# Seven products in the down projection, weight sums by accumulating DMA, whole-unit low parts and a wide input projection, in a one-core macaron block

## The chip, the cores and the metric

The kernel runs on one core of a Trainium2 chip. The metric is the device time of one execution in microseconds. The kernel before took 1792.8 us (median of 3 runs, 1792.15 to 1795.28). One further execution was profiled; everything that is said of stages and instructions comes from that one.

## What is computed

One layer for 256 tokens of width 2048, in float32: a half-step SwiGLU FFN (hidden width 5632), a mixer with two head groups, a second half-step FFN, and a final norm.

```python
x = x + 0.5 * swiglu_ffn(rms_norm(x, ffn1_norm), wg1, wu1, wd1)
z = rms_norm(x, mix_norm) @ w_in                  # 2048 -> 5120
lru_x, lru_gate, sc_b, sc_c, sc_x = split(z, 1024)
h = rg_lru(conv4(lru_x), ...)                     # gates, scan over the 256 tokens
y = concat(rms_norm(h * gelu(lru_gate)), rms_norm(sc_b * conv3(sc_c * sc_x)))
x = x + y @ w_out
x = x + 0.5 * swiglu_ffn(rms_norm(x, ffn2_norm), wg2, wu2, wd2)
out = rms_norm(x, final_norm)
# swiglu_ffn(x, g, u, d) = (silu(x @ g) * (x @ u)) @ d
```

## The kernel before

**Precision.** Every large product is taken in three matmuls on float32r operands. A value v is split into hi (a rounded copy, made by ScalarE) and lo = v - hi (made by VectorE), for weights and activations alike, and hi x hi, lo x hi and hi x lo are added in PSUM. A weight *unit* is a block of 512 rows by 512 columns, loaded by one 1 MB DMA into a tile of 128 x 4 x 512 (`load`, line 155). `parts_of` (line 169) makes its parts in two halves of 128 x 1024 each: hi, then lo, of one half, then of the other. The hi and lo tiles of a half come from a pool of three; inside an FFN two more sets lie in an extra pool.

**Products.** `multiply` (line 197) runs 24 matmuls of 512 columns per unit for both token tiles: all with the weight's hi, then all with its lo. `product` (line 289) is a plain product over units into two PSUM banks. `columns` (line 271) is the input projection: there the weight columns are stationary, and the moving operand is the activation, of which hi lies in columns 0 to 255 of a tile and lo in columns 256 to 511. For each of 4 rows of blocks j and 4 column blocks f it issues three matmuls of 256 columns: hi x hi, hi x lo, lo x hi.

**Seven products.** For gate and up in an FFN, `seven` (line 350) takes two units of K and two units of columns, with the two token tiles, as a 2 x 2 by 2 x 2 block product and does it with 7 products instead of 8 (Strassen in Winograd's form). Each product is one set of 12 matmuls. The other two units of K are added in the plain way (`usual`). The order on TensorE is p0, p4, x(2,1), p5, x(3,1), p6, p2, x(2,0), p3, x(3,0), p1. The products need four sums of weight units: w12 - w11, then w22 - that (both in the tile of w11), w22 - w12, and the second minus w21. VectorE forms all four, on tiles of 128 x 2048. The tiles of w11 and w12 come from a "kept" pool of two, the other six loads go through `raws`, a pool of three. The sums of activations (`seven_of`, line 333) are made once per FFN, and their tiles `vs` hold the same two kept buffers until then. 20 sevens run in all: five for gate and five for up in each FFN.

**Order of an FFN** (`ffn`, line 401): a plain gate product for the first 512 hidden columns, the norm's factor, a plain up product while the parts of x are made, then for s = 0 to 4 a gate seven and an up seven, and after s = 0, 2 and 4 a *down part* (`down`, line 468): four plain products, one per 512 output columns, over the 3, 4 and 4 hidden units that are ready. In FFN 1 the first product is `opening` (line 533): it works through each unit j by j, needing hi and lo of a j together, and turns x meanwhile; inside it the instructions of VectorE, ScalarE and TensorE keep the program's order. Elsewhere a scheduler orders the instructions of each engine when the program is built, and the order is fixed from then on. Each engine executes its own list in that order. All weight loads are issued by SP, in its list's order, and wait there for their buffer.

**Mixer.** `columns` runs ten times; after each of its units a few deferred pieces of element-wise work (convolutions, gates, roots, reciprocals, scan, GeLU) are issued (`pump`). The functions `lru_x`, `lru_gate`, `sc_c`, `sc_x` and `sc_b` take the product from PSUM. Outside the FFNs there is no extra pool.

Of the kernel before, what the change touches and what calls it, by code (L numbers as in the profile page):

```python
# [16 lines left out]
P = 128  # L17
D = 2048
S = 256
# [29 lines left out]
def hybrid_block(ctx: ExitStack, tc: tile.TileContext, a: dict, out: bass.AP):  # L49
# [26 lines left out]
    splits = ctx.enter_context(tc.tile_pool(name="splits", bufs=3))  # L76
# [92 lines left out]
    def parts_of(raw, name, pieces=((0, UK),), split=None):  # L169
        parts = []  # L170
        for h in range(2):
            pool, bufs = splits, 3
            if extra:
                turn_of["split"] += 1
                if turn_of["split"] % 5 > 2:
                    pool, bufs = extra[0], 2
            hi = pool.tile([P, 2, CW], F32R, tag="hi", name=f"hi_{name}_{h}", bufs=bufs)
            lo = pool.tile([P, 2, CW], F32R, tag="lo", name=f"lo_{name}_{h}", bufs=bufs)
            for i, e in pieces:
                if split and i // 2 == h:  # L180
                    split(i)
                o = slice(max(i - 2 * h, 0), min(e - 2 * h, 2))
                if o.start < o.stop:
                    r = raw[:, 2 * h + o.start : 2 * h + o.stop, :]
                    act.copy(hi[:, o, :], r)
                    dve.tensor_tensor(lo[:, o, :], r, f32(hi[:, o, :]), op=ALU.subtract)
            parts.append((hi, lo))
        return [(parts[j // 2][0][:, j % 2, :], parts[j // 2][1][:, j % 2, :]) for j in range(UK)]

    def unit(src, name, pieces=((0, UK),), loaded=None, split=None):  # L190
        return parts_of(load(src, name, pieces, loaded, None), name, pieces, split)
# [119 lines left out]
    class Seven:  # L311
        def __init__(self, name):
            self.tiles = [big(f"sf_{name}_{i}") for i in range(4)]

        def part(self, i):
            o = i % 2 * S
            tile = self.tiles[i // 2][:, :, o : o + S]
            return tile[:, :, :P], tile[:, :, P:]

        def blocks(self, i):  # L320
            hi, lo = self.part(i)
            return [(hi[:, j, :], lo[:, j, :]) for j in range(UK)]

        def put(self, i, v, minus=False):
            hi, lo = self.part(i)
            if minus:
                act.activation(hi, v, AF.Copy, scale=-1.0)
                dve.scalar_tensor_tensor(lo, v, -1.0, f32(hi), op0=ALU.mult, op1=ALU.subtract)
            else:
                act.copy(hi, v)  # L330
                dve.tensor_tensor(lo, v, f32(hi), op=ALU.subtract)

    def seven_of(name, v0, v1, spare):

        sf = Seven(name)
        a11, a21, a12, a22 = v0[:, :, :P], v0[:, :, P:], v1[:, :, :P], v1[:, :, P:]
        sf.put(0, a11)
        dve.tensor_tensor(spare, a21, a22, op=ALU.add)
        sf.put(4, spare)
        dve.tensor_tensor(a21, a11, a21, op=ALU.subtract)  # L340
        dve.tensor_tensor(a11, spare, a11, op=ALU.subtract)
        sf.put(5, a11)
        sf.put(6, a21)
        sf.put(1, a12)
        dve.tensor_tensor(a12, a12, a11, op=ALU.subtract)
        sf.put(2, a12)
        sf.put(3, a22, True)
        return sf

    def seven(w, c0, sf, xp, name, keep, between=None):  # L350
# [3 lines left out]
        def get(u, n, kept=False):  # L354
            src = w[u * UK * P : (u + 1) * UK * P, c0 + n * CW : c0 + (n + 1) * CW]
            return load(src, f"{name}_{u}{n}", kept=kept)

        w11, w12 = get(0, 0, True), get(0, 1, True)
        b2, w22, b3, a2, w21, a3 = get(2, 1), get(1, 1), get(3, 1), get(2, 0), get(1, 0), get(3, 0)
# [6 lines left out]
        def strassen(i, raw, ps, begin=False, end=True):  # L366
            multiply([(ps, sf.blocks(i), begin, end)], parts_of(raw, f"{name}_p{i}"), True)

        def usual(u, raw, n, *targets):

            blk = parts_of(raw, f"{name}_x{u}{n}")
            multiply([(ps, stationary(xp[u - 2], t), b, e) for ps, t, b, e in targets], blk, True)

        strassen(0, w11, a, True)
# [4 lines left out]
        usual(2, b2, 1, (e, 1, True, False), (c, 0, False, False))  # L379
        dve.tensor_tensor(w11, w22, w11, op=ALU.subtract)  # L380
        strassen(5, w11, a)
# [3 lines left out]
        usual(3, b3, 1, (e, 1, False, True), (c, 0, False, False))  # L385
        dve.tensor_tensor(w12, w22, w12, op=ALU.subtract)
        strassen(6, w12, a)
        u3 = snap(a, "u3")
        strassen(2, w22, c)
        usual(2, a2, 0, (d, 0, True, False), (a, 1, False, False))  # L390
        dve.tensor_tensor(w11, w11, w21, op=ALU.subtract)
        strassen(3, w11, a, end=False)
        usual(3, a3, 0, (a, 1, False, True), (d, 0, False, False))
        strassen(1, w21, d)
# [6 lines left out]
    def ffn(tag, norm, after, opening=None):  # L401
        with tc.tile_pool(name=f"ffn{tag}", bufs=1) as fp:
# [4 lines left out]
            def keep(name):  # L407
                return fp.tile([P, CW], F32, tag="keep", name=name, bufs=12)

            hidden = {}  # L410
            waiting = []

            def turn_hidden(u, t, h):
# [10 lines left out]
                dve.tensor_tensor(lo, pt, f32(hi), op=ALU.subtract)  # L424

# [23 lines left out]
            xp = []  # L449
            for u in (0, 1, 2, 3):  # L450
                x = f32(norm.xT[u])
                dve.tensor_tensor(vs[u], x[:, :, :S], x[:, :, S:], op=ALU.add)
                dve.tensor_tensor(vs[u], vs[u], bcs, op=ALU.mult)
                if u == 1:
                    sf = seven_of(f"x{tag}", vs[0], vs[1], keep(f"spare{tag}").rearrange("p (j c) -> p j c", j=UK))
                if u > 1:
                    xp.append(big(f"xp{tag}_{u}"))
                    act.copy(xp[-1][:, :, :S], vs[u])
                    dve.tensor_tensor(xp[-1][:, :, S:], vs[u], f32(xp[-1][:, :, :S]), op=ALU.subtract)
            pu = product(wu, 0, range(4), norm.xT.__getitem__, f"u{tag}_0")  # L460
            for t in range(NT):
                dve.scalar_tensor_tensor(sg[t], pu[t], norm.r[:, t : t + 1], sg[t], op0=ALU.mult, op1=ALU.mult)
                waiting.append((0, t, sg[t]))
# [4 lines left out]
            def down(last):  # L468
                us = sorted(set(hidden) | {w[0] for w in waiting})
                for c in range(NC_D):  # L470
# [4 lines left out]
                    for t in range(NT):  # L475
                        xr = xres[:, t, c * CW : (c + 1) * CW]
                        Engine.pinned = end
                        dve.scalar_tensor_tensor(xr, ps[t], 0.5, xr, op0=ALU.mult, op1=ALU.add)
                        if last:
                            after(c, t)  # L480
                hidden.clear()

            for s in range(5):
                c0 = CW + 2 * s * CW
                g = seven(wg, c0, sf, xp, f"g{tag}_{s}", keep, settle)
                for q in ((1, 1), (0, 1), (1, 0), (0, 0)):
# [4 lines left out]
                    else:  # L491
                        act.activation(g[q], g[q], AF.Silu)
                h = seven(wu, c0, sf, xp, f"u{tag}_{s}", keep)
                for t, n in ((1, 1), (0, 1), (1, 0), (0, 0)):
                    dve.tensor_tensor(g[t, n], h[t, n], g[t, n], op=ALU.mult)
                    waiting.append((1 + 2 * s + n, t, g[t, n]))
# [36 lines left out]
    def opening(wg):  # L533

        ps = [bank(f"ps_g1_0_{t}") for t in range(NT)]
        for u in range(KD // UK):
            src = wg[u * UK * P : (u + 1) * UK * P, :CW]
            if u == 0:
                blk = unit(
                    src, "g1_0_0", ((0, 1), (1, 2), (2, 4)),  # L540
                    lambda i: load_x(1) if i == 1 else None,
                    lambda i: n1.turn((i,) if i < 2 else (2, 3)),
                )
# [32 lines left out]
    with tc.tile_pool(name="mixer", bufs=1) as mp, tc.tile_pool(name="mixw", bufs=2) as mw:  # L576
# [129 lines left out]
        def lru_gate(ps, half):  # L706
            for f in range(4):
                q = 4 * half + f
                g = tmp("g", q, bufs=4)
                dve.tensor_tensor(g, ps[f][:, :S], bc, op=ALU.mult)  # L710
# [3 lines left out]
        def sc_c(ps, half):  # L714
            for f in range(4):
# [3 lines left out]
                act.copy(c[:, 2:], ps[f][:, :S])  # L719
                cc[q] = c  # L720

        def sc_x(ps, half):
            for f in range(4):
                q = 4 * half + f
                c = cc[q][:, 2:]
                dve.tensor_tensor(c, ps[f][:, :S], c, op=ALU.mult)
# [130 lines left out]
```

## Time and profile before

| what | value |
|---|---|
| median of 3 runs | 1792.8 us |
| the profiled execution | 1791.42 us |
| its span (first to last instruction) | 1789.6 us |
| mean granted TensorE clock | 0.997 |
| instructions | 22287 |
| matmuls | 8743 |
| HBM read | 339.82 MB |

The page gives busy time by engine, a chain followed back from the last instruction, and groups of equal instructions. TensorE has two rows: PE for the matmul itself and PEld for loading the stationary operand, which runs beside it. Names in the groups are those of tiles without their numbers: ps_d is a down product's bank, ps_g_a bank a of a gate seven, hi_in and lo_in the parts of an input projection unit. A table by stage, from a query by windows, is shown where it is used; the stages are the opening and the up product (0 to 66 us), a gate and an up seven with a down part of three units (to 217), four sevens and a down part of four units (to 475), the same again (to 733), the input projection (to 973), the output projection (to 1064), and FFN 2 (to 1790).

### The profile page before, as it was taken

What the parts mean: (1) busy time and instruction counts of PE and PEld (TensorE: products, weight loads), DVE (VectorE), ACT (ScalarE), POOL (GpSimd) and SP (SyncE); (2) the same over time, 40 slices, a digit from 0 to 9 for tenths busy, and PEclk for the clock granted to TensorE, in tenths of its full rate; (3) what the DMA queues carried; (4) which work ended last, traced back from release to release, by engine and by line L of the source; (5) the groups of instructions that cost most, each with busy time, mean ns of one, the idle gap of its engine ahead of it and who ended that gap; (6) DMA issues with size and microseconds to landing.
All of it is one profiled execution on the core that took longest, in us unless ns stands there. A gap on an engine that the chain in (4) does not pass through costs nothing.

```text
span 1789.6 us, 22287 instructions
## 1 busy us (share of the span) xinstructions
PE 1765.3 (99%) x8743; PEld 1482.6 (83%) x8743; DVE 1366.0 (76%) x1448; ACT 969.6 (54%) x1204; POOL 6.9 (0%) x32
## 2 busy tenths in 40 slices
PE   7999999999999999999999999999999999999998
PEld 6788888888888888999999887888888888888886
DVE  7996689874789865587886778885889855899854
ACT  6664355653466654465655455653556633656543
POOL 1000000000000000000000000000000000000000
PEclk9999999999999999999999999999999999999999
DMA  7466456575465665455555565575565655555751
GB/s 260 165 213 234 142 190 210 188 250 194 142 203 190 215 230 179 133 172 187 173 182 188 184 203 190 176 258 175 178 205 194 213 191 185 188 188 189 242 205 70
DMA packets 173913, 343.35 MB, mean 192 GB/s; under 512 B 5620, under 2 KB 8048, under 8 KB 173680
## 3 DMA queue, kind: packets, MB, share of 16 engines
q1 hardware_dynamic: 173344, 340.82, 56.1%
q8 instruction: 68, 1.11, 0.3%
q10 hardware_dynamic: 144, 1.05, 0.1%
q14 instruction: 37, 0.30, 0.0%
q0 software_dynamic: 320, 0.07, 0.0%
HBM read 339.82 MB, written 2.10 MB: 191 GB/s over the span
## 4 chain that ended last, share of the span: by engine, by line
PE 92%; DVE 4%; issue 1%; ACT 1%; DMA 1%; SPq 0%; DVEq 0%; ACTq 0%
PE ps_d L42 27%; PE ps_in L42 13%; PE ps_g_a L42 9%; PE ps_u_a L42 9%; PE ps_g_c L42 6%; PE ps_o L42 5%; PE ps_u_c L42 5%; PE ps_u_d L42 5%; PE ps_g_d L42 3%; PE ps_g_e L42 3%; PE ps_u_e L42 2%; PE ps_u L42 2%; PE ps_g L42 2%; DVE raw_u L42 1%; PE ph L42 1%
## 5 line engine op out<-in xcount | busy, mean ns | idle before, releaser
L42 PE MATMUL ps_d<-hi_d,h 128*128 128x512 f32 x1408 | 339.2, 393 | 0.2
L42 DVE TENSOR_TENSOR lo_d<-raw_d,hi_d 128x1024 fp32r<-128x1024 f32 x176 | 210.0, 1221 | 154.9 <-PE ps_d L42 135.6
L42 ACT CAST hi_d<-raw_d 128x1024 fp32r<-128x1024 f32 x176 | 176.8, 1048 | 251.0 <-PE ps_d L42 225.4
L42 PEld LDWEIGHTS ps_d<-hi_d,h 128*128 128x128 f32 x1408 | 263.7, 188 | 58.9 <-ACT h L42 0.8
L42 PE MATMUL ps_in<-xT_nm,hi_in 128*128 128x256 f32 x1280 | 231.4, 283 | 0.0
L42 ACT CAST hi_g_p<-raw_g 128x1024 fp32r<-128x1024 f32 x140 | 142.4, 1050 | 108.4 <-DVE raw_g L42 59.5
L42 PEld LDWEIGHTS ps_in<-xT_nm,hi_in 128*128 128x128 f32 x1280 | 199.6, 192 | 0.2
L42 DVE TENSOR_TENSOR lo_u_p<-raw_u,hi_u_p 128x1024 fp32r<-128x1024 f32 x140 | 166.4, 1219 | 37.6 <-issue 16.9
L42 ACT CAST hi_u_p<-raw_u 128x1024 fp32r<-128x1024 f32 x140 | 143.6, 1047 | 87.1 <-DVE raw_u L42 45.5
L42 DVE TENSOR_TENSOR lo_g_p<-raw_g,hi_g_p 128x1024 fp32r<-128x1024 f32 x140 | 166.3, 1218 | 24.7 <-PE ps_d L42 12.4
L42 PE MATMUL ps_in<-xT_nm,lo_in 128*128 128x256 f32 x640 | 181.1, 283 | 0.0
L42 PE MATMUL ps_d<-lo_d,h 128*128 128x512 f32 x704 | 175.6, 391 | 0.0
L42 PEld LDWEIGHTS ps_d<-lo_d,h 128*128 128x128 f32 x704 | 132.2, 188 | 28.8
L42 DVE TENSOR_TENSOR lo_in<-raw_in,hi_in 128x1024 fp32r<-128x1024 f32 x80 | 97.2, 1217 | 46.8 <-ACT hi_in L42 43.3
L42 ACT CAST hi_in<-raw_in 128x1024 fp32r<-128x1024 f32 x80 | 83.6, 1047 | 84.0 <-PE ps_in L42 74.4
L42 PEld LDWEIGHTS ps_in<-xT_nm,lo_in 128*128 128x128 f32 x640 | 122.7, 192 | 0.0
L42 ACT CAST hi_u_x<-raw_u 128x1024 fp32r<-128x1024 f32 x80 | 82.7, 1051 | 52.2 <-PE ps_u_a L42 17.6
L42 ACT CAST hi_g_x<-raw_g 128x1024 fp32r<-128x1024 f32 x80 | 82.8, 1049 | 43.9 <-PE ps_g_a L42 16.7
L42 DVE TENSOR_TENSOR lo_g_x<-raw_g,hi_g_x 128x1024 fp32r<-128x1024 f32 x80 | 95.8, 1218 | 3.0 <-ACT hi_g_p L42 1.2
L42 DVE TENSOR_TENSOR lo_u_x<-raw_u,hi_u_x 128x1024 fp32r<-128x1024 f32 x80 | 96.0, 1218 | 2.0 <-ACT hi_u_p L42 0.7
L42 DVE TENSOR_TENSOR raw_g<-raw_g,raw_g 128x2048 f32<-128x2048 f32 x40 | 91.3, 2287 | 5.6 <-DMA raw_g<-in_ffn_w_gate_dram 5.2
L42 DVE TENSOR_TENSOR raw_u<-raw_u,raw_u 128x2048 f32<-128x2048 f32 x40 | 91.4, 2285 | 0.8 <-DMA raw_u<-in_ffn_w_up_dram 0.4
(273 smaller groups left out, 2766.4 us busy)
## 6 DMA issues: line engine op xcount, KB each, us to landing
raw_u<-in_ffn_w_up_dram SPq DMA_DIRECT2D x88, 1024.0 KB, 5.4
raw_d<-in_ffn_w_down_dram SPq DMA_DIRECT2D x88, 1024.0 KB, 5.1
raw_g<-in_ffn_w_gate_dram SPq DMA_DIRECT2D x87, 1024.0 KB, 5.2
raw_in<-in_w_in_dram SPq DMA_DIRECT2D x40, 1024.0 KB, 5.2
raw_o<-in_w_out_dram SPq DMA_DIRECT2D x16, 1024.0 KB, 5.1
xres<-in_x_dram SPq DMA_DIRECT2D x4, 512.0 KB, 8.0
fin<-in_final_norm_dram ACTq DMA_DIRECT2D x1, 1024.0 KB, 8.0
out_dram<-xres SPq DMA_DIRECT2D x4, 256.0 KB, 2.6
```

The lines of the kernel that those rows point to most:

```text
L42: ins = getattr(self.engine, name)(*args, **kwargs)
```

## The change

1. **Seven products in the down parts.** Of the four output column blocks, c = 0 and 3 stay plain products. Blocks 1 and 2 are done by one `seven` over the last two hidden units (m, n); the other one or two units are added in the plain way. The activation's parts for it are made in each down part from copies of the turned hidden tiles (`turned`), with tiles from the `keep` pool (13 buffers instead of 12).
2. **Two of four weight sums by DMA.** In every seven, t1 = w12 + w11 and t3 = w12 + w22 are formed by loading w12 into a kept tile (twice) and adding w11 or w22 to it by an accumulating DMA on the POOL queue. The signs of the second column are turned to allow for sums in place of differences. So t1 and t3 hold the kept tiles, w11 goes through `raws`, and a seven has 11 transfers of 1 MB in place of 8. The other two sums stay on VectorE, as additions into t1.
3. **Whole-unit parts.** hi and lo are tiles of a whole unit; hi is still written in two halves, lo in one instruction of 128 x 2048 after both. The pool holds two units, the extra pool of an FFN one more. Only the first unit of the opening keeps its pieces.
4. **Wide input projection.** hi of the weights meets hi and lo of the activation in one matmul of 512 columns; the bank's second half is added to the first when it is taken out (`halves`, a ScalarE copy, and an addition on VectorE).
5. x's parts are made for all four units (`xs`), and the scratch of the POOL queue's DMAs is 2048 bytes instead of 8192.

The core of the diff:

```diff
-    splits = ctx.enter_context(tc.tile_pool(name="splits", bufs=3))
+    splits = ctx.enter_context(tc.tile_pool(name="splits", bufs=2))
...
+    def parts_of(raw, name, pieces=((0, 2), (2, UK)), split=None, minus=False):
+        pool, bufs = splits, 2
+        if extra:
+            turn_of["split"] += 1
+            if turn_of["split"] % 3 == 0:
+                pool, bufs = extra[0], 1
+        hi = pool.tile([P, UK, CW], F32R, tag="hi", name=f"hi_{name}", bufs=bufs)
+        lo = pool.tile([P, UK, CW], F32R, tag="lo", name=f"lo_{name}", bufs=bufs)
+        for i, e in pieces:
+            if split:
+                split(i)
+            if minus:
+                act.activation(hi[:, i:e, :], raw[:, i:e, :], AF.Copy, scale=-1.0)
+            else:
+                act.copy(hi[:, i:e, :], raw[:, i:e, :])
+            if split:
+                dve.tensor_tensor(lo[:, i:e, :], raw[:, i:e, :], f32(hi[:, i:e, :]), op=ALU.subtract)
+        if minus:
+            dve.scalar_tensor_tensor(lo, raw, -1.0, f32(hi), op0=ALU.mult, op1=ALU.subtract)
+        elif not split:
+            dve.tensor_tensor(lo, raw, f32(hi), op=ALU.subtract)
+        return [(hi[:, j, :], lo[:, j, :]) for j in range(UK)]
...
-                    pe.matmul(ps[f][:, :S], hi[:, fs], x[:, :S], start=begin, stop=False)
-                    pe.matmul(ps[f][:, :S], hi[:, fs], x[:, S:], start=False, stop=False)
+                    pe.matmul(ps[f], hi[:, fs], x, start=begin, stop=False)
                     pe.matmul(ps[f][:, :S], lo[:, fs], x[:, :S], start=False, stop=end)
...
+        def sum_of(u, n, u1, n1):
+            raw = load(at(u, n), f"{name}_s{u}{n}{u1}{n1}", kept=True)
+            nc.gpsimd.dma_start(raw, at(u1, n1).rearrange("(j p) c -> p j c", p=P), accum_op=ALU.add)
+            return raw
+        (r0, r1), two = rows, len(xs) > 1
+        w11, t1, t3 = get(r0, 0), sum_of(r0, 1, r0, 0), sum_of(r0, 1, r1, 1)
+        b2, w22 = get(xs[0][0], 1), get(r1, 1)
...
-        dve.tensor_tensor(w11, w12, w11, op=ALU.subtract)
-        strassen(4, w11, c, True)
+        product_of(4, t1, c, True)
...
+                for c in (0, 3):
...
+                    if c == 0:
+                        m, n = us[-2:]
+                        sh = seven_of(
+                            hidden[m], hidden[n], {(t, i): turned[u, t] for t in range(NT) for i, u in ((0, m), (1, n))},
+                            quad(keep(f"hspare{tag}_{m}")),
+                            [[quad(keep(f"hs{tag}_{m}_{i}_{z}", F32R)) for z in range(2)] for i in range(4)],
+                        )
+                        q = seven(wd, (m, n), CW, sh, [(u, hidden[u]) for u in us[:-2]], f"d{tag}_{m}", keep)
+                        for c1 in (1, 2):
+                            for t in range(NT):
+                                update(c1, t, q[t, c1 - 1], (0.5, -0.5)[c1 - 1])
...
+        def halves(ps, name):
+            b = tmp("half", name, bufs=4)
+            act.copy(b, ps[:, S:])
+            return b
...
-                dve.tensor_tensor(z[:, 3:], ps[f][:, :S], bc, op=ALU.mult)
+                b = halves(ps[f], f"x{q}")
+                dve.tensor_tensor(b, ps[f][:, :S], b, op=ALU.add)
+                dve.tensor_tensor(z[:, 3:], b, bc, op=ALU.mult)
```

More of the change, by code (lines that the diff above doesn't have):

```diff
@@ L167, in load, with unit @@
         return raw
[L169 to L191, printed above, removed]
+    def parts_of(raw, name, pieces=((0, 2), (2, UK)), split=None, minus=False):
[20 more added lines that the diff above has]
+        return [(hi[:, j, :], lo[:, j, :]) for j in range(UK)]
+    def unit(src, name):
+        return parts_of(load(src, name, kept=None), name)
     def stationary(tile, t):
@@ L333, in seven_of @@
[L333 to L347, printed above, removed]
-        return sf
@@ L352, in seven, with quad, at, get @@
+    def quad(tile):
+        return tile.rearrange("p (j c) -> p j c", j=UK)
+    def seven(w, rows, c0, sf, xs, name, keep, between=None):
         a, c, e, d = (bank(f"ps_{name}_{n}") for n in "aced")
[L354 to L359, printed above, removed]
+        def at(u, n):
+            return w[u * UK * P : (u + 1) * UK * P, c0 + n * CW : c0 + (n + 1) * CW]
+        def get(u, n):
+            return load(at(u, n), f"{name}_{u}{n}")
+        def sum_of(u, n, u1, n1):
[5 more added lines that the diff above has]
+        b2, w22 = get(xs[0][0], 1), get(r1, 1)
+        b3 = get(xs[1][0], 1) if two else None
+        a2, w21 = get(xs[0][0], 0), get(r1, 0)
+        a3 = get(xs[1][0], 0) if two else None
@@ L384, in seven @@
             between()
-        usual(3, b3, 1, (e, 1, False, True), (c, 0, False, False))
-        dve.tensor_tensor(w12, w22, w12, op=ALU.subtract)
-        strassen(6, w12, a)
+        if two:
+            usual(1, b3, 1, (e, 1, False, True), (c, 0, False, False))
+        product_of(6, t3, a)
         u3 = snap(a, "u3")
[L389 to L394, printed above, removed]
+        product_of(2, w22, c)
+        usual(0, a2, 0, (d, 0, True, False), (a, 1, False, False))
+        dve.tensor_tensor(t1, w21, t1, op=ALU.add)
+        product_of(3, t1, a, end=not two)
+        if two:
+            usual(1, a3, 0, (a, 1, False, True), (d, 0, False, False))
+        product_of(1, w21, d)
         dve.tensor_tensor(u3, u3, s5, op=ALU.add)
@@ L469, in down, with update @@
                 us = sorted(set(hidden) | {w[0] for w in waiting})
-                for c in range(NC_D):
+                def update(c, t, ps, factor=0.5):
+                    xr = xres[:, t, c * CW : (c + 1) * CW]
+                    Engine.pinned = last and tag == 2 and c == NC_D - 1
+                    dve.scalar_tensor_tensor(xr, ps, factor, xr, op0=ALU.mult, op1=ALU.add)
+                    if last:
+                        after(c, t)
+                for c in (0, 3):
                     end = last and tag == 2 and c == NC_D - 1
@@ L538, in opening @@
             if u == 0:
[L539 to L543, printed above, removed]
+                pieces = ((0, 1), (1, 2), (2, 4))
+                raw = load(src, "g1_0_0", pieces, lambda i: load_x(1) if i == 1 else None)
+                blk = parts_of(raw, "g1_0_0", pieces, lambda i: n1.turn((i,) if i < 2 else (2, 3)))
             else:
```

118 lines of the change are left out of this document (65 added, 53 removed).

## Prediction

> **What bounds the kernel now.** I read the page first (busy shares, chain), then a table by stage, then who made TensorE wait, and last the groups by form for the price of one instruction.
>
> ```profile
> PE 1765.3 (99%) x8743; PEld 1482.6 (83%) x8743; DVE 1366.0 (76%) x1448; ACT 969.6 (54%) x1204; POOL 6.9 (0%) x32
> ...
> q1 hardware_dynamic: 173344, 340.82, 56.1%
> ...
> PE 92%; DVE 4%; issue 1%; ACT 1%; DMA 1%; SPq 0%; DVEq 0%; ACTq 0%
> ```
>
> TensorE is busy in 1765.3 of 1789.6 us and carries 92% of the chain, so the time falls only by less work on TensorE or by fewer of the 24.3 us in which it idles. The table by stage (length, then busy us of PE, PEld, DVE, ACT, POOL, granted clock, DMA share, GB/s) shows what stands close behind it: opening, four sevens, a down part, the input projection, the start of FFN 2, the tail.
>
> ```profile
> 0.00:66.00 66.00, 55.89 (x243) 44.33 (x243) 52.07 (x76) 41.84 (x70) 5.89 (x16) 0.97 0.68 240
> ...
> 217.40:392.90 175.50, 175.19 (x778) 142.50 (x777) 156.24 (x138) 106.13 (x122) 0.00 (x0) 1.00 0.59 204
> 392.90:475.40 82.50, 82.50 (x361) 67.57 (x361) 42.70 (x41) 29.98 (x32) 0.00 (x0) 1.00 0.54 179
> ...
> 733.00:973.30 240.30, 240.30 (x1993) 239.48 (x1992) 182.40 (x274) 135.91 (x203) 1.05 (x16) 1.00 0.55 180
> ...
> 1110.00:1204.70 94.70, 92.07 (x410) 74.23 (x408) 83.71 (x73) 56.79 (x66) 0.00 (x0) 1.00 0.62 213
> ...
> 1698.30:1789.60 91.30, 82.60 (x361) 67.26 (x359) 45.45 (x61) 35.71 (x52) 0.00 (x0) 0.97 0.40 139
> ```
>
> In the sevens DVE runs at 156.24 of 175.5 us (89%), and still TensorE loses only 0.3 us there. The granted clock is 1.00 in the stages shown but the first and the last, so it is no term. The waits of TensorE are few:
>
> ```profile
> PE ps_g_c L42 <- ACT hi_g_p L42: 4.3, 2, 2.5
> PE pb_n L42 <- DVE diag_n L42: 2.8, 1, 2.8
> ...
> PE ps_g L42 <- DVE lo_g L42: 1.9, 3, 0.8
> PE ps_u_a L42 <- ACT hi_u_p L42: 0.9, 5, 0.3
> ```
>
> So relieving DVE can win 0.9 us in the sevens; the gain must come from the matmuls.
>
> **Part 1: fewer matmuls.** The chain's long pieces give the spacing of a matmul:
>
> ```profile
> 875.48 97.90 PE ps_in L42 x816
> ...
> 1440.51 82.56 PE ps_d L42 x360
> ```
>
> 82.56 / 360 = 0.2293 us for 512 columns, 97.90 / 816 = 0.1200 us for 256. A seven has 7 products of 12 matmuls where the plain way has 8, so each of the six down parts drops 12 matmuls: 72 x 0.2293 = **16.5 us** off TensorE. In the projection, 640 pairs of 256-column matmuls become 640 of 512 columns: 640 x (0.2400 - 0.2293) = **6.9 us** off; bounds 0 (the wide one costs what the pair does) and 13 us (twice as much, as 0.120 rather than 0.107 per half may go with the weight load, PEld being busy 239.48 of 240.3 us). Total 23.4, and the 0.9 us of small waits in the sevens should go: **-24.3 us**.
>
> **Part 2: sums by DMA.** Two of four sums of 2287 ns leave DVE in each of 20 sevens.
>
> ```profile
> L42 DVE TENSOR_TENSOR lo_d<-raw_d,hi_d 128x1024 fp32r<-128x1024 f32 x176 | 210.0, 1221 | 154.9 <-PE ps_d L42 135.6 <-ACT hi_d L42 14.8 <-ACT hi_in L42 2.5
> ...
> L42 DVE TENSOR_TENSOR lo_in<-raw_in,hi_in 128x1024 fp32r<-128x1024 f32 x80 | 97.2, 1217 | 46.8 <-ACT hi_in L42 43.3 <-PE ps_d L42 3.1
> ...
> L42 DVE TENSOR_TENSOR raw_g<-raw_g,raw_g 128x2048 f32<-128x2048 f32 x40 | 91.3, 2287 | 5.6 <-DMA raw_g<-in_ffn_w_gate_dram 5.2
> L42 ACT CAST hi_in<-raw_in 128x1024 fp32r<-128x1024 f32 x80 | 83.6, 1047 | 84.0 <-PE ps_in L42 74.4 <-PE ps_d L42 3.5 <-DMA raw_in<-in_w_in_dram 2.7
> ...
> L42 DVE RECIPROCAL d<-d 128x256 f32<-128x256 f32 x8 | 13.9, 1741 | 0.0
> ...
> L42 DVE TENSOR_TENSOR cc<-ps_in,cc 128x256 f32<-128x256 f32 x8 | 2.8, 414 | 0.0
> ```
>
> With low parts of 2048 elements (11 x 2.287 instead of 22 x 1.22 us: 1.7 less) that is 6.3 us less DVE per seven, 131 of 175.5 us: hidden under TensorE, worth nothing but safety. The same safety pays for the seven in the down part, where DVE gets 13 operations of 2.287 and eight of about 0.69 us in 180 matmuls (41.3 us): 35.2 us, so it still fits (no cost; at worst some us per part).
>
> The price is in DMA: 11 transfers of 1.049 MB per seven instead of 8, two of them accumulating and issued by POOL, which has only tiny DMAs in this trace. Peak traffic and landing times:
>
> ```profile
> 85.00:90.00 5.00, 5.00 (x23) 4.10 (x22) 5.00 (x9) 1.64 (x2) 0.00 (x0) 1.00 1.05 394
> ```
>
> ```profile
> raw_u<-in_ffn_w_up_dram SPq DMA_DIRECT2D x88, 1024.0 KB, 5.4
> ...
> rows_many<-in_lru_b_a_dram POOLq DMA_DIRECT2D x1, 4.0 KB, 5.9
> ```
>
> At 394 GB/s a transfer takes 2.66 us of all 16 queues. A seven with its transposes takes 175.5 / 4 = 43.9 us, so 9 plain ones leave 43.9 - 9 x 2.66 = 20.0 us, 10 us for each accumulating one, 3.7 times a plain one. Nearest row: the plain transfer, 2.66; far end: POOL's 5.9 plus two plain landings of 5.4, 16.7 us with nothing overlapping. I take 5.3 of transfer time and 8 us to landing (both operands are moved, by the first row): no stall. "Collectives: The Full Stack" of the Trainium skill (section "The bandwidth ceiling: the fold count and why AG ≠ RS ≠ AR") says that an add in a DMA halves the rate because it needs two source reads; no run here shows it yet. By it a seven's DMA would be 13 x 2.66 = 34.6 of 43.9 us, and the sum stays.
>
> Latency: the built order puts the load for t1 behind the previous seven's p6, for t3 behind its p3. Counted in matmuls, p6's parts can be done some 17 us into a seven and p3's some 28, and TensorE wants the next t1 at 43.9 + 2.7 and the next t3 at 43.9 + 19: about 30 us each, into which load 5.4 + accumulate 8 + hi 1.05 fit twice. SP's later loads (b2, w22, ...) stand behind these two in its queue, but by then the buffers that they need are not free either. Not so in each FFN's first seven: both buffers are held by the scaled inputs until DVE has made the parts, and p4 now waits for load and accumulate (5.4 + 8) where it waited for load and a DVE sum (5.4 + 2.29). DVE's preparation gets about 2 us shorter and t1 takes the buffer that frees first (2.3 us earlier). 4.3 us of waits become about 7: **+3 us** (bounds 0 and +20, by the ends above).
>
> **Part 3: whole-unit low parts.** In the opening every j needs its low part at once, in program order.
>
> ```profile
> 12.97 2.00 ACT L42 CAST hi_g<-raw_g 128x1024 fp32r<-128x1024 f32 x2 [0.32 <-DMA raw_g<-in_ffn_w_gate_dram]
> ...
> 19.60 2.01 ACT L42 CAST hi_g<-raw_g 128x1024 fp32r<-128x1024 f32 x2
> ```
>
> ```profile
> 21.50 2.35 DVE L42 TENSOR_TENSOR lo_g<-raw_g,hi_g 128x1024 fp32r<-128x1024 f32 x2
> ```
>
> ```profile
> 15.38 0.45 PE L42 MATMUL ps_g<-lo_g,xT_n 128*128 128x512 f32 x1
> ...
> 22.77 0.50 PE L42 MATMUL ps_g<-lo_g,xT_n 128*128 128x512 f32 x1 [0.79 <-DVE lo_g L42]
> ```
>
> Unit 1: hi ends at 14.97, a whole low part at 17.26, TensorE wanted it at 15.38: +1.9. Units 2 and 3: half a low part was there at 22.65, a whole one is at 21.61 + 2.29 = 23.9: +1.25 each. Behind it, the built order puts a low part of the next product ahead of diag on DVE, and its buffer is free only when the opening's last matmul is done: 2 x 1.05 + 2.29 + 0.28 = 4.7 us, where TensorE waited 2.8: +2. Together **+6.4 us** (bounds 3 and 8).
>
> In the projection the low part is also needed within one matmul of a unit's start. Before, a half took 1.05 + 1.22 = 2.27 and could be made two halves (5.76 us) ahead: 3.5 us of slack. Now there are two whole buffers, a unit lasts 16 x (0.2293 + 0.1200) = 5.59 and takes 2 x 1.047 + 2.287 = 4.4: 1.2 us of slack. DVE gains 40 operations of about 0.414 us and loses 5.7 us of low parts: 182.4 + 16.6 - 5.7 = 193 of 233 us. That fits on the mean (4.8 of 5.59 per unit), but in the built order some twelve of the 40 units have 6 to 7 us of DVE work between two low parts (gates, the reciprocals of 1.741 us). Adding up what goes beyond budget and slack gives **+6 us**; bounds 0 and 22 (each unit's chain 4.4 with one reciprocal in the way, 6.14 - 5.59 = 0.55, x 40).
>
> **The sum**: -24.3 + 3 + 6.4 + 6 = -8.9. The profiled execution took 1791.4 us (span 1789.6 and 1.8 around it), 1.4 below the median shown: 1791.4 - 8.9 = 1782.5, said as **1783 us**, 0.5% faster.
>
> **Rivals.** *All hidden*: first sevens and projection cost nothing, 1791.4 - 24.3 + 6.4 = 1773.5, and 1767 if the opening hides as well. For it: DVE idles 40 us in the projection. Against: 1.2 us of slack. *Low parts bind in the projection*: towards the bound of 22 in place of 6, the time is 1789 to 1799. For it: the stage table's 83% and the small slack. *Slower: the accumulating DMAs saturate the queues in the sevens.* Place: t1 and t3 of each seven; it decides from 3.7 times a plain transfer (10 us). Half a plain transfer beyond, 4.2 times, costs 2 x 1.33 x 20 = 53 us: 1836; one beyond, 1889. For it: no such DMA in the trace, and POOL's 5.9 us for 4 KB. Against: 10 us is far from the nearest row. *It doesn't do what it says*: the wide matmul saves nothing, 1790; the count of the down parts is certain, since the built program has 72 fewer.
>
> **How the numbers follow.** What differs from 1792.8 by less than 0.2% (3.6 us) can't be told from no change. Forecast (1774 to 1789) 0.50; all hidden 0.12; low parts or the wide matmul take the gain back 0.20, of which 0.13 within 0.2% and 0.07 slower; saturated DMA 0.18. Faster 0.62, same 0.13, slower 0.25. Range 1768 to 1830: below it lies the end of "all hidden" (0.03), above it most of the saturation (0.12).
>
> **What would show it.** Right: 8020 or so matmuls; ps_d's time down by 16.5 us; the projection near 239 us (240.3 - 6.9 + 6) with waits for lo_in; p4's wait in the two first sevens near 3.5 us each; TensorE over 99% busy in the other sevens; the accumulating DMA landing in about 8 us. Wrong: TensorE waiting for hi of p4 or p6 in every seven with DMA share near 1 (saturation); landing times of the plain loads above 9 us; a projection over 245 us (low parts) or under 235 (all hidden).

## The result and the profile after

The changed kernel took **1840.6 us** (median of 4 runs, 1837.3 to 1852.6), the kernel before beside it 1792.5 us (median of 4): a ratio of 1.0277 [1.0257, 1.0297], 2.8% slower. The forecast was 1783 us, 0.5% faster, with a range from 1768 to 1830: the time lies above the range, and on the slower side. The profiled execution took 1839.95 us with a span of 1838.2 us, against 1789.6 before.

The page of the changed kernel: busy time by engine, the two DMA queues that carry the weights (packets, MB, share of the 16 engines' span), the chain, and how long the 1 MB transfers took from issue to landing.

```profile
PE 1760.0 (96%) x8031; PEld 1449.0 (79%) x8031; DVE 1385.9 (75%) x1169; ACT 1045.3 (57%) x1342; POOL 74.4 (4%) x84
...
q1 hardware_dynamic: 187072, 368.08, 58.7%
q0 software_dynamic: 27776, 54.60, 16.6%
...
PE 76%; DMA 13%; DVE 6%; ACT 3%; issue 2%; SPq 0%; DVEq 0%; ACTq 0%; POOLq 0%
...
raw_u<-in_ffn_w_up_dram SPq DMA_DIRECT2D x78, 1024.0 KB, 6.9
...
raw_u_s<-in_ffn_w_up_dram POOLq DMA_DIRECT2D x20, 1024.0 KB, 12.4
```

TensorE has 712 matmul rows fewer (72 from the down parts, 640 from the projection) and is busy only 5.3 us less; it idles 78.2 us in place of 24.3. The chain, 92% TensorE before, has 13% of DMA in it. The waits of TensorE (total, times, longest):

```profile
PE ps_u_c L42 <- ACT s_u L42: 22.9, 10, 6.6
PE ps_g_c L42 <- ACT hi_g_p L42: 15.7, 2, 8.8
PE ps_g_c L42 <- ACT s_g L42: 8.1, 5, 3.1
PE ps_g L42 <- DVE lo_g L42: 5.1, 3, 2.0
PE pb_n L42 <- DVE diag_n L42: 4.5, 1, 4.5
```

The first and third are new: 31.0 us in 15 of the 20 gate and up sevens, waiting for a *copy* (s5, which takes PSUM bank c out before the product x01 adds to it), not for a weight. The second is the wait for p4 in the first seven of each FFN (4.3 before). The last two are the opening and the norm behind it. One of the copy waits in the timeline, in the fourth up seven of FFN 1 (start, length, engine, operation; in brackets the idle time ahead and what ended it):

```profile
546.56 1.99 ACT L42 CAST hi_u_p<-raw_u_s 128x1024 fp32r<-128x1024 f32 x2 [6.12 <-DVE raw_u_s L42]
548.46 1.05 ACT L42 ACTIVATE hi_u_x<-raw_u 128x1024 fp32r<-128x1024 f32 x1
549.41 0.56 ACT L42 COPY s_u<-ps_u_c 128x512 f32<-128x512 f32 x1
...
544.18 2.29 DVE L42 TENSOR_TENSOR raw_u_s<-raw_u,raw_u_s 128x2048 f32<-128x2048 f32 x1 [4.89 <-DMA raw_u<-in_ffn_w_up_dram]
546.39 2.28 DVE L42 SCALAR_TENSOR_TENSOR lo_u_x<-raw_u,hi_u_x 128x2048 fp32r<-128x2048 f32 x1
...
541.48 1.97 PE L42 MATMUL ps_u_e<-hi_u_x,x 128*128 128x512 f32 x8
550.03 2.50 PE L42 MATMUL ps_u_c<-hi_u_x,x 128*128 128x512 f32 x5 [6.58 <-ACT s_u L42]
```

Read it backwards. Bank c was complete at 541.5, so s5 could have run at once. But on ScalarE it stands behind the high part of p5, that waits for VectorE's sum t1 += w22, and that waited 4.89 us for the plain load of w22; half the high part of x11 stands ahead of it too. On VectorE the low part of x01, which TensorE wants next, stands behind the same sum. What a late load should have delayed was p5, which comes 16 matmuls after the point at which TensorE stopped; through two in-order lists it stopped everything. The built lists say the same for all: in the kernel before no high part of p5 stands ahead of s5 in any seven; after the change both halves do in 18 of the 20 gate and up sevens and in all six in the down parts, and in the 18 half a high part of x11 with them.

The load itself was slow. It was issued at 533.7 us, when its buffer came free, and landed 10.4 us later; an accumulating DMA was under way from 532.4 to 543.5. From 505 to 552 us the plain up loads took as long on the median (over the whole run it is 6.9, in the kernel before 5.4, and without the second transfers, below, 5.2):

```profile
raw_u<-in_ffn_w_up_dram SPq DMA_DIRECT2D x5, 1024.0 KB, 10.4
```

The stall also costs afterwards. By windows (length; then busy us of PE, PEld, DVE, ACT, POOL; granted clock, DMA share, GB/s):

```profile
536.00:543.50 7.50, 7.45 (x33) 5.76 (x31) 3.21 (x3) 3.38 (x5) 0.00 (x0) 1.00 1.08 269
543.50:550.00 6.50, 0.00 (x0) 0.00 (x0) 5.82 (x3) 3.44 (x5) 0.00 (x0) 0.78 0.43 158
550.00:557.00 7.00, 6.97 (x22) 5.57 (x23) 4.25 (x3) 2.93 (x3) 0.00 (x0) 0.71 0.80 254
```

The clock falls inside the wait and is 0.71 in the 7 us behind it, where 22 matmul rows pass instead of 33 in a like time.

### The profile page after: what moved, and what is told of

It reads as the page before. It is cut to its first block, busy times and chain, and to the rows that moved or that the text cites. A ratio compares the mean times of both kernels' runs of the same rounds, so it can differ in the third digit from the quotient of the medians.

```text
span 1838.2 us, 20486 instructions
## 1 busy us (share of the span) xinstructions
PE 1760.0 (96%) x8031; PEld 1449.0 (79%) x8031; DVE 1385.9 (75%) x1169; ACT 1045.3 (57%) x1342; POOL 74.4 (4%) x84
## 3 DMA queue, kind: packets, MB, share of 16 engines
q0 software_dynamic: 27776, 54.60, 16.6%
HBM read 421.61 MB, written 2.10 MB: 231 GB/s over the span
## 4 chain that ended last, share of the span: by engine, by line
PE 76%; DMA 13%; DVE 6%; ACT 3%; issue 2%; SPq 0%; DVEq 0%; ACTq 0%; POOLq 0%
PE ps_in L42 12%; PE ps_d L42 11%; PE ps_g_a L42 7%; PE ps_u_a L42 6%; DMA raw_u<-in_ffn_w_up_dram 6%; PE ps_g_c L42 5%; PE ps_d_a L42 5%; DMA raw_g<-in_ffn_w_gate_dram 5%; PE ps_o L42 5%; PE ps_u_c L42 5%; PE ps_d_c L42 3%; PE ps_u_d L42 3%; PE ps_g_e L42 3%; PE ps_d_d L42 2%; DMA raw_g_s<-in_ffn_w_gate_dram 2%; PE ps_u_e L42 2%
## 5 line engine op out<-in xcount | busy, mean ns | idle before, releaser
L42 PE MATMUL ps_in<-xT_nm,hi_in 128*128 128x512 f32 x640 | 225.6, 397 | 0.0
L42 PE MATMUL ps_d<-hi_d,h 128*128 128x512 f32 x704 | 170.6, 393 | 2.8 <-DVE h L42 2.2
L42 PEld LDWEIGHTS ps_d<-hi_d,h 128*128 128x128 f32 x704 | 131.5, 188 | 32.9 <-DVE h L42 3.0
L42 ACT CAST hi_d<-raw_d 128x1024 fp32r<-128x1024 f32 x88 | 87.8, 1047 | 83.9 <-PE ps_u_d L42 23.7
L42 DVE TENSOR_TENSOR lo_g_p<-raw_g_s,hi_g_p 128x2048 fp32r<-128x2048 f32 x40 | 91.5, 2288 | 55.8 <-ACT hi_g_p L42 53.4
L42 DVE TENSOR_TENSOR lo_d<-raw_d,hi_d 128x2048 fp32r<-128x2048 f32 x44 | 100.7, 2290 | 30.6 <-ACT hi_d L42 30.5
L42 DVE TENSOR_TENSOR lo_u_p<-raw_u_s,hi_u_p 128x2048 fp32r<-128x2048 f32 x40 | 91.6, 2289 | 35.2 <-ACT hi_u_p L42 29.5
L42 DVE TENSOR_TENSOR lo_in<-raw_in,hi_in 128x2048 fp32r<-128x2048 f32 x40 | 91.4, 2285 | 33.4 <-ACT hi_in L42 28.6
L42 ACT CAST hi_g_p<-raw_g 128x1024 fp32r<-128x1024 f32 x60 | 61.1, 1052 | 48.5 <-PE ps_g_a L42 16.8
L42 PE MATMUL ps_d<-lo_d,h 128*128 128x512 f32 x352 | 87.6, 390 | 0.0
L42 ACT CAST hi_u_p<-raw_u 128x1024 fp32r<-128x1024 f32 x60 | 61.0, 1050 | 43.6 <-PE ps_u_a L42 31.4
L42 DVE TENSOR_TENSOR lo_u_p<-raw_u,hi_u_p 128x2048 fp32r<-128x2048 f32 x30 | 68.7, 2288 | 16.8 <-ACT hi_u_p L42 16.7
## 6 DMA issues: line engine op xcount, KB each, us to landing
raw_g_s<-in_ffn_w_gate_dram POOLq DMA_DIRECT2D x20, 1024.0 KB, 11.5
raw_u_s<-in_ffn_w_up_dram POOLq DMA_DIRECT2D x20, 1024.0 KB, 12.4
```

Source lines behind the costliest of these rows:

```text
L42: ins = getattr(self.engine, name)(*args, **kwargs)
```

## The experiments

The **order theory**: the loss comes from late loads *and* from what stands behind them on ScalarE and VectorE. The **transfer theory** (my rival): accumulating DMAs take so much of the queues that the late loads set the pace whatever stands where. A **buffer theory**: w11 is now a seventh load through three raw buffers, so loads start late. Ratios are against the kernel before, run beside each.

**All sums on VectorE (dve_sums).**

```diff
-        w11, t1, t3 = get(r0, 0), sum_of(r0, 1, r0, 0), sum_of(r0, 1, r1, 1)
+        t1 = w11 = load(at(r0, 0), f"{name}_{r0}0", kept=True)
+        t3 = load(at(r0, 1), f"{name}_{r0}1", kept=True)
...
+        dve.tensor_tensor(t1, t3, t1, op=ALU.add)
         product_of(4, t1, c, True)
...
+        dve.tensor_tensor(t3, w22, t3, op=ALU.add)
         product_of(6, t3, a)
```

> The changed kernel with the two sums of each seven that go by an accumulating DMA formed on VectorE again (w12 is added to w11 in place, w22 to w12 in place, eight loads instead of nine, no POOL transfer); the sevens in the down parts, the whole-unit low parts, the signs and the wide projection stay. If part 2, in whichever way, costs what was lost: the copy waits of the sevens (31.0 us of TensorE waiting for s_u and s_g) and the first sevens' 15.7 us for hi_g_p go back to the 4.3 us of before, and the clock stays at 1.00: 1792.5 - 16.5 (matmuls) - 8.5 (wide projection, by the 0.3467 us that a pair took after) + 6 (opening) = 1773.5, so 1770 to 1785. If the loss sits in the other parts (sevens in the down parts, whole-unit low parts): 1825 to 1840. A third case: VectorE is too full with 15 operations of 2.29 us in a down part's seven, and waits for low parts appear there: 1785 to 1800.

Measured: 1780.2 us, 0.9928 [0.9912, 0.9945]. So part 2 costs 60.3 us and turns a gain into the loss; copy waits are 0.2 us, hi_g_p 1.6 us. The full VectorE did not bind.

**Second transfers left out (no_second).**

```diff
-            nc.gpsimd.dma_start(raw, at(u1, n1).rearrange("(j p) c -> p j c", p=P), accum_op=ALU.add)
```

> The changed kernel without the 52 second transfers: t1 and t3 are w12 alone, so both sums are left out and what is computed is not the reference's; the order of the lists (copy s5 behind the high part of p5) and the seven loads of a block through the three shared raw buffers stay as in the changed kernel. Transfer theory (DMA time of the second transfers and what queues behind them is what makes w22 late): 1772 to 1785, copy waits under 5 us. Buffer theory (a seventh load through three buffers makes w22's load start late, whatever the second transfers do): copy waits of 20 us and more, 1810 to 1835. Order theory in its strict form (the lists alone, however early w22 lands): also 1810 and more.

Measured: 1771.8 us, 0.9878 [0.9864, 0.9893], no copy wait at all, though the lists have the p5 parts ahead of s5 in 18 sevens as well and seven loads still go through three buffers. The buffer theory falls, and so does an order theory that needs no late load; it takes the second transfers, and so far the transfer theory stands. The page has the matmuls of the changed kernel at a nearly clean price (granted clock 0.995), and the up loads' landing:

```profile
PE 1740.9 (98%) x8031; PEld 1442.0 (81%) x8031; DVE 1387.2 (78%) x1169; ACT 1046.0 (59%) x1342; POOL 6.9 (0%) x32
...
raw_u<-in_ffn_w_up_dram SPq DMA_DIRECT2D x78, 1024.0 KB, 5.2
```

This splits the difference of the two spans, 1838.2 - 1770.3 = 67.9 us: TensorE is busy 1760.0 - 1740.9 = 19.1 us longer on the same matmuls, and idles the other 48.8. The first part is half clock: the trace's clock record has 41.0 us more of it than in no_second ahead of the tail, and about half of that is lost.

**The same transfers without the add (plain_second).**

```diff
-            nc.gpsimd.dma_start(raw, ..., accum_op=ALU.add)
+            nc.gpsimd.dma_start(raw, ...)
```

> The changed kernel with the 52 POOL transfers made plain (they overwrite instead of adding, so both sums are left out and what is computed is not the reference's); same bytes from memory, same queue, same waits, same order. If it is the adding that costs (5.6 us of all queues per MB against 2.9): q0's time falls from 16.6% to about 8.5% of the span, the transfers land in 6 to 8 us instead of 11.5 to 12.4, and the time falls to 1778 to 1795. If it is the second transfer as such, started only when the first has landed and in the same queues: the landing falls little and the time stays at 1815 to 1840.

Measured: 1797.4 us (1788.8 to 1802.5, 10 runs; its profiled one, span 1787.0, is at the low end), 1.0020 [1.0004, 1.0036]: a little above the range for the add as the cost, far below the one for the second transfer as such, so both cost something.

```profile
q0 software_dynamic: 14464, 54.60, 8.3%
...
raw_u_s<-in_ffn_w_up_dram POOLq DMA_DIRECT2D x20, 1024.0 KB, 8.0
```

A plain MB on this queue costs 0.083 x 1787.0 / 54.6 = 2.72 us of the 16 engines, an accumulating one 0.166 x 1838.2 / 54.6 = 5.59: 2.06 times. "Collectives: The Full Stack" of the Trainium skill ("The bandwidth ceiling: the fold count and why AG ≠ RS ≠ AR") has an add halve the rate in a ring of cores; the same factor comes out here. Its reason, two source reads, is not shown here: both runs read the same 421.61 MB from memory. With this build's lists the add costs 43 us and the second transfer as such 26.

**Orders put back, in part (both_first).** `issue_after` puts what is issued in its block behind the given instruction in that engine's list (names shortened).

```diff
+        with tc.issue_after(low_part_of_x01):
             dve.tensor_tensor(t1, w22, t1, op=ALU.add)
-        product_of(5, t1, a)
+        with tc.issue_after(copy_s5):
+            product_of(5, t1, a)
```

> The changed kernel with nothing but two orders put back: on ScalarE the copy s5 of PSUM c stands ahead of the high part of p5, on VectorE the low part of x01 ahead of the sum t1 += w22, as in the kernel before; every transfer and its place in the queues stays. Order theory: TensorE's stall comes from the copy and the low part standing behind work that waits for w22's late load; w22 itself is wanted only 24 matmuls (5.5 us) later, so of the 31.0 us of copy waits some 5 to 10 remain, as waits for p5's parts, and of the clock loss behind them (about 1.3 us per us waited) as much: 1800, range 1795 to 1812. Transfer theory (the late transfers alone set the pace, whatever stands in the lists): the waits move from the copy to hi or lo of p5 and stay near 31 us: 1830 to 1842.

Measured: 1837.3 us, 1.0241 [1.0214, 1.0267]: by the letter of the expectation the order theory had lost.

```profile
PE ps_u_c L42 <- ACT s_u L42: 18.8, 6, 5.8
PE ps_g_c L42 <- ACT hi_g_p L42: 15.7, 2, 8.7
PE ps_g_c L42 <- ACT s_g L42: 11.7, 4, 3.6
```

But the waits had not moved behind p5, as the transfer theory wants; they were still waits for the copy. The timeline shows what stood ahead of it now, half a high part of x11, which stood there in the changed kernel as well and whose load (b3) comes later still:

```profile
548.17 0.59 ACT L42 COPY s_u<-ps_u_a 128x512 f32<-128x512 f32 x1 [0.82 <-PE ps_u_a L42]
554.09 1.06 ACT L42 ACTIVATE hi_u_x<-raw_u 128x1024 fp32r<-128x1024 f32 x1 [5.33 <-DMA raw_u<-in_ffn_w_up_dram]
555.05 0.57 ACT L42 COPY s_u<-ps_u_c 128x512 f32<-128x512 f32 x1
```

The built lists have that half ahead of s5 in ten of the 20 gate and up sevens (the next expectation says eight; ten is right), and TensorE's ten copy waits lie in exactly these ten.

**The copy ahead of all of it (all_first).**

```diff
         with tc.issue_after(copy_s5):
             product_of(5, t1, a)
+            u2 = snap(a, "u2")
+            if between:
+                between()
+            if two:
+                usual(1, b3, 1, (e, 1, False, True), (c, 0, False, False))
+            product_of(6, t3, a)
```

> The changed kernel with the copy s5 of PSUM c ahead of every high part of p5, x11 and p6 on ScalarE in all 26 sevens (the version before this one left half a high part of x11 ahead of it in 8 of the 20 gate and up sevens and lost 30.5 us in copy waits, all in sevens of that kind), and the low part of x01 ahead of the sum t1 += w22 on VectorE; transfers and queues stay. Order theory: the late loads hurt only through what stands behind them in the two lists; copy waits go from 31.0 us to near 0 and nothing takes their place, since the x01 product gives 24 matmuls (5.5 us) of cover: 1840.5 - 31 - some 10 of half clock = 1800, range 1792 to 1810; the first sevens' 15.7 us for hi_g_p stay. Transfer theory: the late loads set the pace, and the waits come back behind the next product that needs a late load (hi or lo of p5, x11 or p6): 1825 to 1842.

Measured: 1795.7 us, 1.0020 [1.0007, 1.0033]: 44.8 us less than the changed kernel, with every transfer in place. TensorE's longest waits, the landing times and queue share from the page, and most of the first stage of four sevens by windows:

```profile
PE ps_g_c L42 <- ACT hi_g_p L42: 16.8, 2, 9.1
PE ps_g L42 <- DVE lo_g L42: 5.8, 3, 2.0
```

```profile
q0 software_dynamic: 27776, 54.60, 17.1%
...
raw_u<-in_ffn_w_up_dram SPq DMA_DIRECT2D x78, 1024.0 KB, 8.0
```

```profile
240.00:424.00 184.00, 184.00 (x823) 151.57 (x822) 147.65 (x96) 114.42 (x135) 10.37 (x8) 1.00 0.88 269
```

The loads land later than in the changed kernel (8.0 against 6.9 us) and the queues are no less busy (q0 17.1% against 16.6%; all 16 engines 0.88 in this window), and TensorE does not idle in 184 us. Outside the first gate seven of each FFN, neither late loads alone (here) nor the lists alone (no_second) cost anything that shows; together they cost 45 us. That sum nearly closes: the copy waits were 33.1 us (2.1 of them in a down part), and half clock ahead of the tail falls from 54.6 to 30.7 us, of which half is time lost. The transfer theory falls for all sevens but those first two. Which of the two lists mattered more, ScalarE's or VectorE's, was not separated: both were put back together.

**The first sevens on VectorE (first_dve).** all_first with VectorE's sums in the first gate seven of each FFN (`by_dve` chooses the lines of dve_sums).

```diff
-                g = seven(wg, (0, 1), c0, sf, xs, f"g{tag}_{s}", keep, settle)
+                g = seven(wg, (0, 1), c0, sf, xs, f"g{tag}_{s}", keep, settle, by_dve=s == 0)
```

> The version with accumulating DMAs and the copy s5 first (1795.7 us), with the two sums of the first gate seven of each feed-forward layer formed on VectorE (its two sums need no accumulating DMA; the other 24 sevens keep theirs). If what is left of the loss is the chain of load, accumulating DMA and high part behind the buffers that the scaled inputs free late: the two waits for hi_g_p (16.8 us) fall to about 2 to 4, the 20.4 us of half clock behind them go (up to 10 us of work): 1776, range 1770 to 1783. If the accumulating DMAs of the other sevens still cost by making plain loads late: above 1785.

Measured: 1778.9 us, 0.9916 [0.9902, 0.9931], the wait for hi_g_p 2.4 us. So the other 16.8 us of part 2 were the chain of load, accumulating DMA and high part in two places. The 24 sevens that keep their accumulating DMAs now cost nothing that shows beside dve_sums (1780.2).

**Half-unit low parts in the opening (dve_halves, first_dve_halves).** Units 1 to 3, in dve_sums and in first_dve:

```diff
-                blk = unit(src, f"g1_0_{u}")
+                blk = parts_of(load(src, name, kept=None), name, split=lambda i: None)
```

> The version with all sums on VectorE (1780.2 us) with half-unit low parts in units 1 to 3 of the opening, as before the change; whole units everywhere else. The opening's three waits for lo_g (5.3 us) shrink to the 1.9 us of before, with at most one half-clock spell less behind them: 1774 to 1778. If the opening's time is set by the loads and not by the low parts, nothing changes: 1779 to 1781.

> The version before, with half-unit low parts in units 1 to 3 of the opening as well: 5 us less than it, as between the two versions with all sums on VectorE (1780.2 to 1775.1): 1771, range 1766 to 1778. Against the version with all sums on VectorE and these halves (1775.1) it then tells what accumulating DMAs are worth where they hurt nothing: my forecast said nothing (VectorE is hidden either way), so within 4 us of it.

Measured: 1775.1 us, 0.9902 [0.9880, 0.9924], and 1773.6 us, 0.9886 [0.9869, 0.9903]: 5.1 and 5.3 us less. The two versions differ by 1.5 us, within their runs' spread: harmless accumulating DMAs are worth nothing measurable.

**The wide projection alone, on the kernel before (wide_only).** Only `columns` and the five functions that take its product are changed.

> The kernel before with the wide input projection alone (512-column matmuls on the high parts, the halves added by ScalarE and VectorE), half-unit low parts and all else as before. By the spacing after the change (a pair of wide and narrow matmul in 0.3467 us, 55.47 us for 320, against 0.3600 before): 640 x 0.0133 = 8.5 us less: 1784 to 1786 beside 1792.5 to 1793.2. By my forecast's 6.9 us: 1786. If the extra halves make ScalarE or VectorE late: 1788 to 1793.

Measured: 1788.8 us, 0.9975 [0.9966, 0.9985], 4.4 us less. A chain piece of 48 pairs, before and then in this run:

```profile
742.33 17.28 PE ps_in L42 x144
```

```profile
742.84 16.65 PE ps_in L42 x96
```

A pair is the work on hi and lo of one block, three matmuls before and two here; 0.3600 us a pair becomes 0.3469. From the first long piece of ps_in to the start of ps_o it is 237.5 us before (735.7 to 973.2) and 232.5 here (736.3 to 968.8), a wait for diag_nm of 1.6 us that was not there before included. The time lies in the expectation's third range, short of both the 8.5 and the 6.9 us.

**Down parts as plain products (down_plain)** in dve_sums, `for c in range(NC_D)` with `product` alone; and **only the three-unit ones plain (dve_down4)** in dve_halves:

```diff
-                for c in (0, 3):
+                for c in (0, 3) if len(us) > 3 else range(NC_D):
```

> The version with all sums on VectorE (1780.2 us) and the six down parts as plain products of eight quarter products each instead of sevens. By the count, 72 matmuls come back: + 72 x 0.2293 = 16.5 us, less the 2.9 us that TensorE waits for h in the down parts and the half clock behind it: 1793 to 1797. If the sevens in the down parts gain less than their count (VectorE too full, waits for parts): 1783 to 1790.

> The version with all sums on VectorE and half-unit low parts in the opening (1775.1 us), with the two down parts of three units as plain products and sevens only in the four of four units. By the stages of the traces the sevens in the three-unit parts cost 1.2 and 0.6 us instead of gaining 2.75 each (TensorE waits 1.4 us for h there, and half clock follows): 1775.1 - 1.8 = 1773, range 1769 to 1777. By the count of matmuls alone 24 x 0.2293 = 5.5 us come back: 1780.6.

Measured: down_plain 1788.2 us, 0.9976 [0.9965, 0.9988], 8.0 more than dve_sums, not 16.5, and inside the second range. The stages tell where; first dve_sums (first sevens with the three-unit part, then four sevens with a four-unit part), then down_plain:

```profile
72.20:226.90 154.70, 151.66 (x662) 122.81 (x662) 142.20 (x118) 95.63 (x112) 0.00 (x0) 0.99 0.56 191
226.90:480.30 253.40, 253.40 (x1126) 208.45 (x1125) 219.58 (x135) 148.03 (x171) 0.00 (x0) 1.00 0.59 199
```

```profile
73.40:226.90 153.50, 151.77 (x673) 123.86 (x673) 120.47 (x98) 83.26 (x94) 0.00 (x0) 1.00 0.57 192
226.90:482.80 255.90, 255.90 (x1138) 210.62 (x1137) 196.25 (x117) 135.91 (x153) 0.00 (x0) 1.00 0.59 197
```

The four-unit part gains 2.5 us of the 2.75 counted, the three-unit part loses 1.2. There TensorE waits 1.42 us for the parts of h, which do not make it wait in down_plain, and the clock is 0.99. dve_down4: 1773.7 us, 0.9886 [0.9872, 0.9901], 1.4 below dve_halves instead of 5.5 above it; that is inside dve_halves' spread (1770.6 to 1780.0), so the two sevens of three units are worth about nothing rather than a proven loss.

**All together (all_together):** first_dve_halves with three-unit parts plain.

> Accumulating DMAs in all sevens but the first gate seven of each layer, the copy s5 first, half-unit low parts in the opening, and plain products in the two down parts of three units. If the four effects add up: 1773.6 - 1.4 (what the plain three-unit parts gave with all sums on VectorE, 1775.1 to 1773.7) = 1772, range 1768 to 1776. If the three-unit sevens were no loss here, because VectorE has two sums less in them: 1774 to 1779.

Measured: 1772.5 us (1770.1 to 1775.5), 0.9886 [0.9869, 0.9903]: the fastest, 21 us under the kernel before and 68 under the changed one, with 46 MB still added by DMA, though not told apart from dve_down4 and first_dve_halves.

## Why the prediction was wrong

- **The step that failed** is part 2's "no stall" for the accumulating DMAs in the sevens, costed at 0. Its transfer price was right (5.3 us estimated, 5.6 measured; DMA share under 1 on the mean). I then asked whether t1 and t3 are there in time, and counted "about 30 us each" of slack, which was there too: after the first sevens the big waits are not for their high parts. What I did not price is the other loads. I wrote that SP's later loads lose nothing because their buffers are not free either; in the stall shown the start was as I wrote, but they land in 6.9 instead of 5.4 us on the median (this one in 10.4), and behind the one for w22 the new build had put s5 and x01's low part. Before, s5 stood ahead. I had followed SP's order and not ScalarE's and VectorE's around the banks. Price: 44.8 us (changed kernel against all_first) of the 57.6 between forecast and time.
- **First sevens**, +3 with bounds 0 and +20: right mechanism, wrong size. The waits are 15.7 us instead of "about 7", and undoing them gave 16.8 us with the clock. The landing was 11.5 to 12.4 us by the medians and 13.5 and 13.4 in these two places, not 8, and behind the two waits the clock is halved for 6.8 and 10.2 us.
- **The granted clock "is no term"** failed with the stalls: 19.1 us.
- **Sevens in the down parts**, -16.5: measured -8.0. The count of matmuls was right; the four-unit parts gave 2.5 of 2.75 us each by the stages, the three-unit ones nothing. "It still fits" was right of VectorE's mean, but not of the start of a three-unit part.
- **Wide projection**, -6.9: the spacing was right or better (640 x 0.0131 = 8.4 by the chain piece); 5.0 us of the stage and 4.4 of the time came.
- **Low parts of the projection**, +6: measured nothing. From the first long piece to ps_o, dve_sums takes 231.2 us (736.3 to 967.5) with whole units, wide_only 232.5 with halves; the changed kernel waits 1.2 us for lo_in. With the wide matmuls the stage is 6.3 us shorter in dve_sums than before, where I had forecast 0.9. Why the sum over the units whose VectorE work runs over its budget came out too high was not tested; it left out that idle time between them can take such work back.
- **Opening**, +6.4 with bounds 3 and 8: measured +5.1 and +5.3 by putting halves back. Right; in the changed kernel the waits for lo_g grew by 3.2 us and the one for diag by 1.7.
- **The slower rival** named accumulating DMAs and 1836 us, close to the time, but by a mechanism that did not happen: it wanted 4.2 times a plain transfer (2.06 on the same queue), and TensorE waiting for the high parts of p4 or p6 in every seven. Its other signs did appear in places: the median landing of a plain load stayed under 9 us, but 65 of the 292 FFN loads took longer (2 of 266 before), and the DMA share was 1.08 just ahead of the stall shown. That is not what cost the time by itself, since in all_first 79 loads take over 9 us. So the nearness of 1836 is no support for its reason.

Left open: why the scheduler moved s5. Where t1 comes straight from transfers, with or without the second one, it did so in 18 of the 20 gate and up sevens, all but the first of each FFN, and in dve_sums in two of the 20; what it reckoned with was not tried.

## What to carry to other kernels

A late transfer and an in-order list can together cost what neither costs alone: ask not only what waits for the data, but what stands behind that wait on each engine, above all a copy that empties a PSUM bank TensorE is about to add to. When a change alters where data comes from, compare the built lists of every engine, not of the DMA queue alone; holding the copy and VectorE's low part ahead was worth 45 us here. A stall's price is its length and the half clock behind it.

## What the runs showed of the hardware

- **The clock after short waits.** In the trace's clock record of the changed kernel half-clock spells last 3.4, 6.8 or 10.2 us and sum to 54.6 us ahead of the tail, in the kernel before one of 3.4. "TensorE: Matmul & The Clock Gate" of the Trainium skill, section "Part 1: The HAM clock gate (the "warmup" mystery)", has the clock at half rate when TensorE was idle and at full rate when it was busy, by a free-running window of about 3.4 us. The lengths of the spells, one, two or three times 3.4 us, agree. The idle window that it asks for ahead of half rate was not needed here: spells followed waits of 1.21, 2.13 and 2.29 us as well as of 8.75, and one wait of 3.31 us had none.
- **An accumulating DMA into SBUF** takes 5.6 us of the 16 engines per MB against 2.7 for a plain one on the same queue, and lands 12.4 us after its issue against 8.0 (up weights). In all_first, where the copy no longer stood behind late loads, TensorE did not idle in 184 us of sevens at a DMA share of 0.88.
